# Mixture of experts on one core: thirteen groups of a heavy and one or two light experts instead of fifteen pairs, and weights fetched into idle places before the first

## The chip, the cores and the metric

The kernel runs on one core of one Trainium2 chip. The metric is the device time of one execution in microseconds (us), here the median of three runs. A profiled execution of the same program gives the rows quoted below; its span is the time from the first to the last instruction on the core.

## The reference

One decoder block on 512 tokens of 1024 values, float32: RMSNorm, projection, differential attention beside an S5 state-space branch, output projection, residual; then a mixture of 32 experts, four per token, and a final RMSNorm. What bears on the change is the mixture:

```python
def _moe(h, w_router, b_router, w1, b1, w2, b2):
    logits = (hf @ w_router + b_router).astype(jnp.float32)
    top_val, top_idx = lax.top_k(logits, TOP_K)      # 4 of 32
    gates = jax.nn.softmax(top_val, axis=-1)
...
    def expert_block(args):
        xb, e = args
        gu = xb @ w1[e] + b1[e]                      # 1024 -> 2048
        gate, up = jnp.split(gu, 2, axis=-1)
        gate = jnp.minimum(gate, SWIGLU_LIMIT)
        up = jnp.clip(up, -SWIGLU_LIMIT, SWIGLU_LIMIT)
        glu = gate * jax.nn.sigmoid(SWIGLU_ALPHA * gate)
        return ((up + 1.0) * glu) @ w2[e] + b2[e]    # 1024 -> 1024
```

The output is the sum over a token's four experts, each times its gate, added to the residual.

## The kernel before

**Weights.** Each expert has twelve chunks of 128 x 2048 float32 (1.049 MB): eight of w1 ("up") and four of w2 ("down"). All 32 experts are read once, 384 chunks. They land in seven raw tiles (three `raw2`, four `raw`, `weight_tile`), all loaded by SyncE in one fixed order (`chunks`, `chunk`, `load`), so that a load waits until the chunk seven loads earlier has been used.

**Ranks.** After routing, experts are ranked by the number of their tokens. Ranks 0 to 12 are heavy: a block of 128 rows, weights split into a high half (`hA`, by ScalarE, L926) and a low half (`hB`, by VectorE, L927), three products per weight (`up_heavy`, `down_heavy`), at most three chunks split ahead (`AHEAD`, three `hA` and three `hB` tiles). Ranks from 13 on are light: 64 rows, or 32 for the ranks in `SMALL`, multiplied straight from the raw tile in float32 (`up_light`, `down_light`). Rank 31 is a light block whose expert is always expert 0, so its weights can be loaded before routing is known; rank 0 has an extra block of 32 rows, X. The matmuls of all of these stand at L1078 (`Stream.matmul`). A block's rows are found by four slot matmuls (L975), gathered from `h2_d` in DRAM by GpSimd (L1028), and transposed by TensorE (L1050 light, L1061 heavy). The bias of a light expert is four matmuls (L1094). Between up and down TensorE transposes the gated activations (L1191 light, L1157 heavy). Results are added to `acc` by scatter matmuls (L1351), 16 for a heavy block, 8 for a light one, and VectorE's additions (L1354); a group issues those of the group before it.

**Order.** The expert stage is written as sixteen pairs. Pair 0 (`first_pair`) is ranks 31 and 13, all light. Pairs 1 to 6 and 8 to 14 are a heavy and a light expert: heavy up, light up, heavy down, light down. Pairs 7 and 15 are two light experts each (19 and 20, 26 and 27). Within `pair` the next pair's blocks are prepared (`block_of`, `prepare2`), and `later` places three pieces of other work: tables in pair 3 and the two halves of the down bias (`down_bias`, eight matmuls in all at L1300) in pairs 5 and 7.

**The start.** Chunks 0 to 6 of expert 0 are loaded long before the experts begin. Chunks 7 to 9 go into split tiles after the last write of `h2_d` (L948, kept there by `issue_after`). `out_tile` is the output projection of one quarter of the tokens: it writes x1 (L684) and h2 (L692) to DRAM. `out_weights` splits its weights into the same ring of `hA` and `hB` tiles. When all is routed, VectorE and TensorE make the table of ranks `perm`, the biases by rank `bT` (sixteen matmuls, L1246) and the list `ordi` of experts by rank (L1250, L1254), which SyncE reads (L1493) before it can load any expert but expert 0.

Of the kernel before, what the change touches and what calls it, by code (L numbers as in the profile page):

```python
# [11 lines left out]
I32 = mybir.dt.int32  # L12
# [21 lines left out]
NHEAVY = 13  # L34
SMALL = (28, 29, 30)
NRAW = 7
AHEAD = 3
# [9 lines left out]
def decoder_block_kernel(ctx: ExitStack, tc: tile.TileContext, A, out):  # L47
# [26 lines left out]

    turn_hl = dict(A=-1, B=0)
# [461 lines left out]
    wo = A['w_out'][0].rearrange("(k p) n -> p k n", p=P)  # L537
    WOH, WOL = [], []

    def out_weights():  # L540
        for kp2 in range(4):
            w = raw_tile()
            if kp2 < 2:
                SP.dma_start(w.rearrange("p (k n) -> p k n", n=D), wo[:, 2 * kp2:2 * kp2 + 2])
            else:
                for k in range(2):
                    r0 = (2 * kp2 + k) * P
                    SP.dma_start(w[:, k * D:(k + 1) * D],
                                 A['w_out'][0, r0:r0 + P].rearrange("(g c) n -> c g n", c=CW))
            wh, wl = hl_tile("A"), hl_tile("B")  # L550
            ACT.activation(wh, w, AF.Copy)
            V.tensor_tensor(wl, w, wh.bitcast(F32), op=OP.subtract)
            WOH.append(wh.rearrange("p (k n) -> p k n", n=D))
            WOL.append(wl.rearrange("p (k n) -> p k n", n=D))

# [102 lines left out]
    last_rows = [None]  # L658

    def out_tile(t):  # L660

# [201 lines left out]

    def load(eidx, c):

        w = weight_tile()
        SP.dma_start(w, w1r[eidx, c] if c < 8 else w2r[eidx, c - 8])
        return w
# [90 lines left out]
    def ps_m():  # L959
        return mp.tile([P, 512], F32, name="pm", tag="pm", bufs=2)  # L960
# [75 lines left out]
    def rows_of(B):  # L1036
# [3 lines left out]
        V.tensor_scalar(B.oT, iot, B.meta[:, 1:2], None, op0=OP.is_equal)  # L1040

    def prepare2(B):

        light, xg, n, selc = B.light, B.xg, B.n, B.selc
        if light:
            xT, B.aT = (mo.tile([P, KT * 64], F32, name=z + "Tl", tag=z + "Tl", bufs=2)[:, 0:KT * n]
                        .rearrange("p (k q) -> p k q", q=n) for z in "xa")
            pt = ps_m()
# [136 lines left out]

    def act_light(B, half, late=False):
        if B.n == 32:
            return act_small(B, late) if half == 0 else None
# [45 lines left out]
    perm = mo.tile([P, NE], F32, name="perm")  # L1234
    V.tensor_scalar(perm, iot[:, 0:NE], key[:, 2:3], None, op0=OP.is_equal)

    permr = mo.tile([P, NE], F32R, name="permr")
    V.tensor_copy(permr, perm)
    bT = mo.tile([P, 2, 2, 4, NE], F32, name="bT")
    for u in range(2):  # L1240
# [6 lines left out]
        ACT.activation(bT[:, u].rearrange("p h k r -> p (h k r)"), pb_[:, 0:256], AF.Copy)  # L1247
    po = ps_m()
    for i in range(2):
        PE.matmul(po[0:1, i * NE:(i + 1) * NE], ecol[0:32, i:i + 1], perm[0:32], start=True, stop=True)  # L1250
    orow = mo.tile([1, 2, NE], F32, name="orow")
    V.tensor_copy(orow, po[0:1, 0:64])
    ordi = mo.tile([1, NE], I32, name="ordi")
    V.tensor_copy(ordi, orow[:, 0])  # L1254
    for i in range(2):
# [227 lines left out]

    rest = iter((13, 14, 15, 16, 28, 17, 18, 19, 20, 29, 21, 22, 23, 30, 24, 25, 26, 27))
# [11 lines left out]

    chunks = [(31, c) for c in range(12)] + [(pairs[0][1], c) for c in range(12)]
    chunks += [(r, c) for h, l in pairs[1:]
               for r, cs in ((h, range(8)), (l, range(8)), (h, range(8, 12)), (l, range(8, 12))) for c in cs]
    place = {x: i for i, x in enumerate(chunks)}  # L1500
    weights = [early[c] for c in range(10)]

    def chunk(r, c):
        while len(weights) <= place[r, c]:
            z = chunks[len(weights)]
            weights.append(load(expert_id(z[0]), z[1]))
        return weights[place[r, c]]
# [5 lines left out]

    def next_pair(n):
        return pairs[n + 1] if n + 1 < len(pairs) else (None, None)

# [4 lines left out]
    def down_last(n, rl, L):  # L1521

        nh = next_pair(n)[0]
        gl = [ps_g()]
        for c in range(8, 12):
            down_light(L, c - 8, chunk(rl, c), gl)
            if nh is not None and nh < NHEAVY and c >= 9:
                split_ahead(nh, c - 9)
        return gl

    def first_pair(B):

        (rb, rl), (nh, nl) = pairs[0], pairs[1]
        nxt = {}
# [22 lines left out]

    def pair(n, B, X, L):

        (rh, rl), (nh, nl) = pairs[n], next_pair(n)  # L1560
        nxt = {}
        g = [ps_g() for _ in range(2 if B.light else 4)]
        gx = [ps_g()] if X else None
        for c in range(8):
            w = chunk(rh, c)
            if B.light:
                up_light(B, c, w, g)
            else:
                wh, wl = split(w)
                up_heavy(B, c, wh, wl, g)  # L1570
                if X:
                    up_light(X, c, w, gx)
                if c + AHEAD < 8:
                    split_ahead(rh, c + AHEAD)
            if c == 1 and nh is not None:
                nxt['h'] = block_of(nh)
            elif c == 3 and nl is not None:
                nxt['l'] = block_of(nl)
            elif c == 2 and n in later:
                later[n]()  # L1580
            elif c >= 5:
                scatter(c - 5, False)
        if B.light:
            leave_light(B, g)
        else:
            for half in range(2):
                act_heavy(B, half, g[half], g[2 + half])
        if X:
            leave_light(X, gx)
        gl = [ps_g() for _ in range(L.n // 32)]  # L1590
        for c in range(8):
            up_light(L, c, chunk(rl, c), gl)
            if c == 4:
                for half in range(2):
                    act_light(B, half) if B.light else turn_heavy(B, half)
                if X:
                    for half in range(2):
                        act_light(X, half)
            if c >= 5 and not B.light:
                split_ahead(rh, 8 + c - 5)  # L1600
        leave_light(L, gl, not B.light)
        g = [ps_g() for _ in range(1 if B.light else 2)]
        gx = [ps_g()] if X else None
        for c in range(8, 12):
            w = chunk(rh, c)
            if B.light:
                down_light(B, c - 8, w, g)
            else:
                wh, wl = split(w)
                down_heavy(B, c - 8, wh, wl, g)  # L1610
                if X:
                    down_light(X, c - 8, w, gx)
            if c == 8:
                for half in range(2):
                    act_light(L, half, not B.light)
                if not B.light:
                    split_ahead(rh, 11)
            elif c == 9:
# [9 lines left out]
        if X:  # L1628
            gated(X, gx)
        gl = down_last(n, rl, L)  # L1630
        if nh is None:
            beyond(L.last)
        gated(L, gl, nh is not None and nh < NHEAVY)
# [6 lines left out]
    for n in range(1, len(pairs)):  # L1640
        blocks = pair(n, *blocks)

# [82 lines left out]
```

## Time and profile before

| what | value |
|---|---|
| runs (us) | 1430.03, 1433.55, 1435.22; median 1433.55 |
| profiled execution | 1432.14 us, span 1430.2 us |
| mean granted TensorE clock | 0.956 of full speed |
| front, to the first expert matmul | 335.65 us |
| pair 0, to the first matmul of pair 1 | 62.65 us |
| pairs 1 to 15 | 1012.0 us |
| tail | 19.9 us |
| moved by DMA | 477.68 MB, mean 334 GB/s |

The stages are cut at the first expert matmul of each pair on TensorE, as read in the timeline. "Busy" of TensorE is modelled at the ends of matmuls, so that a stretch can be called busy in which some waiting is hidden.

### The profile page before, as it was taken

The page shows a single profiled execution, that of the slowest core. Times are in us where ns is not written, and L with a number is a line of the kernel's source. Part 1 is how long each engine was busy: PE and PEld are TensorE (multiplying, and loading weights), DVE is VectorE, ACT ScalarE, POOL GpSimd, SP SyncE. Part 2 cuts the span into 40 slices and gives each one's busy share as a digit, 9 for nine tenths or more (in the row PEclk, how much of TensorE's full clock was granted, in tenths as well). Part 3 has the DMA queues.
Part 4 walks back from the last instruction along what each step waited for, and adds up shares of the span by engine and source line. Part 5 has one row for each costly group of instructions (what it writes and reads, how often), then busy time and mean ns, then how long its engine had stood idle before and what let it go on. Part 6 is the DMA issues. An engine that isn't in the chain of part 4 may idle for free. (4 is left out here: it accounts for less than half of the span.)

```text
span 1430.2 us, 18851 instructions
## 1 busy us (share of the span) xinstructions
PE 1347.5 (94%) x6888; PEld 836.7 (59%) x6888; DVE 934.5 (65%) x1557; ACT 567.2 (40%) x681; POOL 133.1 (9%) x97
## 2 busy tenths in 40 slices
PE   3999999998999999999999999899999999999996
PEld 1778764774365656657565446565655565656532
DVE  4899546653285867778676537685867586867524
ACT  6442327321245354545254114445343354453312
POOL 1020101222010101102010000020101010201000
PEclk8999858997999999999999999999999999999998
DMA  9745647748899999999799999999997899999994
GB/s 273 245 124 195 204 148 211 254 140 321 362 400 407 361 406 366 403 379 415 307 395 367 409 393 409 417 377 388 365 401 275 346 377 383 372 394 363 416 415 176
DMA packets 103603, 477.68 MB, mean 334 GB/s; under 512 B 24739, under 2 KB 41987, under 8 KB 52307
## 3 DMA queue, kind: packets, MB, share of 16 engines
q1 hardware_dynamic: 90416, 459.86, 82.5%
q0 software_dynamic: 4432, 14.05, 2.9%
q10 hardware_dynamic: 8658, 2.52, 0.8%
q8 instruction: 56, 0.92, 0.3%
q14 instruction: 41, 0.33, 0.1%
HBM read 467.73 MB, written 8.67 MB: 333 GB/s over the span
## 5 line engine op out<-in xcount | busy, mean ns | idle before, releaser
L927 DVE TENSOR_TENSOR hB<-raw,hA 128x2048 fp32r<-128x2048 f32 x156 | 355.3, 2287 | 54.8 <-ACT hA L926 54.3
L926 ACT ACTIVATE hA<-raw 128x2048 fp32r<-128x2048 f32 x156 | 295.0, 1911 | 139.2 <-PE pg L1078 75.5
L1078 PE MATMUL pg<-raw,xTl 128*64 128x512 f32 (+1 forms) x1272 | 263.1, 600 | 0.1
L1078 PE MATMUL pg<-hA,xT 128*128 128x512 f32 x832 | 229.0, 400 | 0.0
L1078 PEld LDWEIGHTS pg<-hA,xT 128*128 128x128 f32 x832 | 157.1, 190 | 42.6 <-issue 6.0
L1028 POOL DMA_INDIRECT xg<-h_d,tid x32 | 83.1, 2596 | 874.5 <-DVE oh L971 730.7
L1078 PEld LDWEIGHTS pg<-raw,xTl 128*64 128x64 f32 (+1 forms) x1272 | 76.6, 132 | 146.5 <-issue 141.0
L1078 PE MATMUL pg<-hA,aT 128*128 128x512 f32 x416 | 139.7, 416 | 7.2 <-ACT hA L926 7.2
L1078 PE MATMUL pg<-hB,xT 128*128 128x512 f32 x416 | 126.1, 404 | 12.0 <-DVE hB L927 11.8
L1078 PE MATMUL pg<-raw,aTl 128*64 128x512 f32 (+1 forms) x752 | 127.5, 524 | 0.0
L1354 DVE TENSOR_TENSOR acc<-acc,pm 128x512 f32<-128x512 f32 x128 | 83.4, 683 | 42.0 <-PE pm L1351 41.5
L1078 PEld LDWEIGHTS pg<-hA,aT 128*128 128x128 f32 x416 | 80.1, 195 | 35.2 <-ACT hA L926 13.9
L1078 PEld LDWEIGHTS pg<-hB,xT 128*128 128x128 f32 x416 | 76.3, 190 | 36.8 <-DVE hB L927 20.1
L1078 PE MATMUL pg<-hB,aT 128*128 128x512 f32 x208 | 79.9, 411 | 5.3 <-DVE hB L927 5.3
L1078 PEld LDWEIGHTS pg<-raw,aTl 128*64 128x64 f32 (+1 forms) x752 | 41.0, 127 | 68.1 <-issue 63.4
L1351 PE MATMUL pm<-yy,oT 128*128 128x512 f32 x208 | 66.4, 408 | 1.0 <-ACT hA L926 0.4
L1141 ACT ACTIVATE gm<-gm 128x512 f32<-128x512 f32 x26 | 16.4, 631 | 124.3 <-DVE gm L1139 124.3
L1194 DVE TENSOR_TENSOR gb<-pm,bT 128x512 f32<-128x512 f32 x32 | 21.2, 688 | 63.0 <-PE pm L1191 62.2
L1162 DVE TENSOR_TENSOR aT<-pm,aT 128x512 fp32r<-128x512 f32 x26 | 16.8, 686 | 61.9 <-ACT aT L1161 61.9
L1326 ACT ACTIVATE yyl<-gy 64x512 fp32r<-64x512 f32 (+1 forms) x48 | 26.8, 559 | 70.9 <-DVE gy L1318 70.2
L1167 ACT ACTIVATE gu<-pg 128x512 f32<-128x512 f32 x36 | 20.1, 588 | 86.7 <-PE pg L1078 86.7
L1351 PE MATMUL pm<-yyl,oT 128*128 128x512 f32 (+1 forms) x152 | 51.8, 423 | 1.4 <-DVE acc L1354 0.8
(495 smaller groups left out, 1799.8 us busy)
## 6 DMA issues: line engine op xcount, KB each, us to landing
raw<-in_w_dram SPq DMA_DIRECT2D x381, 1024.0 KB, 9.4
raw<-in_w_ada_dram SPq DMA_DIRECT2D x16, 1024.0 KB, 4.8
raw<-in_w_ada_dram SPq DMA_DIRECT2D x16, 512.0 KB, 5.6
raw<-in_w_in_dram SPq DMA_DIRECT2D x8, 1024.0 KB, 6.5
xt<-in_x_dram SPq DMA_DIRECT2D x4, 512.0 KB
raw<-in_w_out_dram SPq DMA_DIRECT2D x2, 1024.0 KB
raw<-in_w_out_dram SPq DMA_DIRECT2D x4, 512.0 KB, 14.6
xh<-in_x_dram SPq DMA_DIRECT2D x4, 512.0 KB, 4.1
```

The costliest lines, as they stand in the source:

```text
L926: splits['hi'] = ACT.activation(wh, w, AF.Copy)
L927: splits['lo'] = V.tensor_tensor(wl, w, wh.bitcast(F32), op=OP.subtract)
L1028: POOL.indirect_dma_start(out=xg[0:n], out_offset=None, in_=h2_d[:, :], in_offset=bass.IndirectOffsetOnAxis(ap=tid[0:n, :1], axis=0))
L1078: ins = PE.matmul(*args, **kw)
L1141: ACT.activation(gm, gm, AF.Gelu_apprx_sigmoid)
L1162: V.tensor_tensor(lo, u4, hi.bitcast(F32), op=OP.subtract)
L1167: left = ACT.activation(gu, pss[half], AF.Copy)
L1194: biased = V.tensor_tensor(gb, p4, bT[:, :, half, :, B.rank:B.rank + 1].to_broadcast([P, 2, 4, 64]), op=OP.add)
L1326: high = ACT.activation(hi, g, AF.Copy)
L1351: PE.matmul(ps[n], oT, rows, start=(seen[n] == 1), stop=(2 * seen[n] == len(mms)))
L1354: V.tensor_tensor(acc[:, t, ns], acc[:, t, ns], ps[n], op=OP.add)
```

## The change

The expert stage becomes fourteen groups. Group 0 is as before (31 and 13). The other thirteen have one heavy expert and one light expert, and in groups 2, 4, 7 and 12 a second light expert (`TWO_LIGHT`). The order there is: heavy up, first light up, heavy down, second light up, first light down, second light down. The pairs of two light experts are gone. The second half of the down bias moves from the light pair 7 to group 8, a heavy one.

Nine chunks are fetched ahead: chunks 7 to 10 of expert 0 are issued inside the last `out_tile`, right behind its matmuls and ahead of its x1 and h2 writes; chunk 11 after routing; and the first four chunks of the expert of rank 13 go into a split tile and the places of `yy`, `xT` and `aT`, which the first heavy group uses later. For that, `out_weights` takes its four parts in the order 2, 3, 0, 1 and the turn of the split tiles is shifted. The list `ordi` is made ahead of the biases by rank, and the tile `aTl` is taken when it is filled.

```diff
+TWO_LIGHT = (2, 4, 7, 12)
...
-        for kp2 in range(4):
+        for kp2 in (2, 3, 0, 1):
...
+    def ahead(cs):
+
+        with tc.issue_after(last_rows[0].ins):
+            for c in cs:
+                early[c] = split_tile("AB"[c % 2], F32)
+                SP.dma_start(early[c], w1r[0, c] if c < 8 else w2r[0, c - 8])
...
             PE.matmul(pss[n], ml[:, k, ts], wh[:, ns], start=False, stop=(k == 3))
+        if t == NT - 1:
+            ahead(range(7, 11))
...
-    with tc.issue_after(last_rows[0].ins):
-        for c in range(7, 10):
-            early[c] = split_tile("AB"[c % 2], F32)
-            SP.dma_start(early[c], w1r[0, c] if c < 8 else w2r[0, c - 8])
+    ahead(range(11, 12))
...
-    pairs = [(r, next(rest)) for r in (31, 1, 2, 3, 4, 5, 6)]
-    pairs.append((next(rest), next(rest)))
-    pairs += [(r, next(rest)) for r in (7, 8, 9, 0, 10, 11, 12)]
-    pairs.append((next(rest), next(rest)))
+    groups = [(31, [next(rest)])]
+    for n, r in enumerate((1, 2, 3, 4, 5, 6, 7, 8, 9, 0, 10, 11, 12), 1):
+        groups.append((r, [next(rest) for _ in range(2 if n in TWO_LIGHT else 1)]))
...
+    spare = [lambda: split_tile("A", F32)]
+    spare += [lambda n=n: mo.tile([P, 2048], F32, name=n, tag=n, bufs=1) for n in ("yy", "xT", "aT")]
+    weights = [early[c] for c in range(12)]
...
+        if M:
+            g = [ps_g() for _ in range(M.n // 32)]
+            for c in range(8):
+                up_light(M, c, chunk(rm[0], c), g)
+            leave_light(M, g)
+            g = [ps_g()]
+            for c in range(8, 12):
+                down_light(L, c - 8, chunk(rl, c), g)
+                if c == 8:
+                    for half in range(2):
+                        act_light(M, half)
+            gated(L, g)
+            L, rl = M, rm[0]
         gl = down_last(n, rl, L)
...
-    later = {3: beyond_tables, 5: lambda: down_bias(0), 7: lambda: down_bias(1)}
+    later = {3: beyond_tables, 5: lambda: down_bias(0), 8: lambda: down_bias(1)}
```

SyncE's queue at the end of the front, before: the last x1 write (`x_d`) and h2 write (`h_d`), three loads of expert 0 into split tiles, the first part of `acc`, two loads into raw tiles, and the reading of `ordi`.

```order
L684 DMA x_d<-xh 128x1024
L692 DMA h_d<-t_2583 128x1024
L948 DMA hB<-in_w_dram 128x2048
L948 DMA hA<-in_w_dram 128x2048
L948 DMA hB<-in_w_dram 128x2048
L1011 DMA acc<-x_d 128x1024
L867 DMA raw_2985<-in_w_dram 128x2048
L867 DMA raw_2991<-in_w_dram 128x2048
L1493 TENSOR_LOAD ordi
```

The same place in the changed program:

```order
L665 DMA hB<-in_w_dram 128x2048
L665 DMA hA<-in_w_dram 128x2048
L665 DMA hB<-in_w_dram 128x2048
L665 DMA hA<-in_w_dram 128x2048
L693 DMA x_d<-xh 128x1024
L701 DMA h_d<-t_2583 128x1024
L665 DMA hB<-in_w_dram 128x2048
L1016 DMA acc<-x_d 128x1024
L1501 TENSOR_LOAD ordi
```

Four loads stand ahead of the two writes, one instead of three between the h2 write and `acc`, and `ordi` is read before any further load; the loads into `hA`, `yy`, `xT` and `aT` follow it.

TensorE's queue in group 2 of the changed program, from the end of the heavy down matmuls (`hA`, `hB` with `aT`) to the second light's up and the first light's down (raw tiles with `xTl` and `aTl`); L1085 is the former L1078, L1057 the former L1050, L1200 the former L1191, L980 the former L975:

```order
L1085 MATMUL pg<-hA,aT 128x512 x2
L1057 MATMUL pm<-ident,xg 128x32 x8
L1085 MATMUL pg<-raw,xTl 64x512 x16
L1085 MATMUL pg<-raw_4213,xTl 64x512 x4
L1085 MATMUL pg<-raw_4219,xTl 64x512 x4
L1085 MATMUL pg<-raw_4225,xTl 64x512 x4
L1085 MATMUL pg<-raw,xTl 64x512 x4
L1200 MATMUL pm<-ident,gu 128x128 x8
L980 MATMUL pm<-tb,oh 128x66
L1085 MATMUL pg<-raw,aTl 64x512 x4
```

Before, light down matmuls followed the heavy down ones at once; now eight chunks of the second light's up stand between, with its transposes behind them.

VectorE's queue before the first heavy group, before: `sel` is the bias selector of that group, `ms` and `tid` the slots of a later block, L927 the low half.

```order
L1065 TENSOR_TENSOR xT<-pm,xT 128x512
L1054 TENSOR_SCALAR sel<-ones,perm 128x128
L977 COPY ms<-pm 128x66
L971 TENSOR_SCALAR oh<-iot,posr 128x128
L979 CAST tid<-ms 128x1
L1406 TENSOR_TENSOR meta<-ms 128x1
L1032 COPY meta<-ms 128x1
L971 TENSOR_SCALAR oh<-iot,posr 128x128 x3
L927 TENSOR_TENSOR hB<-raw_3185,hA 128x2048
```

And in the changed program, where L936 is the low half, L1327 and L1338 the gate products of the light expert:

```order
L1072 TENSOR_TENSOR xT<-pm,xT 128x512
L936 TENSOR_TENSOR hB<-raw_3184,hA 128x2048
L936 TENSOR_TENSOR hB<-raw_3194,hA 128x2048
L936 TENSOR_TENSOR hB<-raw,hA 128x2048
L1327 SCALAR_TENSOR_TENSOR gy<-pg,meta,g2l 128x512
L1061 TENSOR_SCALAR sel<-ones,perm 128x128
L1338 TENSOR_TENSOR yyl<-gy,yyl 64x512 x2
```

Three low halves have moved ahead of the selector and of the slots of the next blocks.

## Rows read from the trace of the kernel before

**Rows 1.** The page: busy time and share of an engine, and the weights' queue.
```profile
PE 1347.5 (94%) x6888; PEld 836.7 (59%) x6888; DVE 934.5 (65%) x1557; ACT 567.2 (40%) x681; POOL 133.1 (9%) x97
...
q1 hardware_dynamic: 90416, 459.86, 82.5%
```

**Rows 2.** Windows of five pairs (2, 5, 7, 8, 15).
```profile
core 0: us, PE busy (x) PEld busy (x) DVE busy (x) ACT busy (x) POOL busy (x), PEclk, DMA share, GB/s
...
464.30:532.20 67.90, 66.63 (x311) 42.42 (x310) 49.02 (x65) 30.53 (x27) 5.37 (x2) 1.00 0.96 382
...
662.90:738.50 75.60, 73.48 (x320) 44.12 (x317) 53.01 (x73) 33.10 (x31) 8.31 (x2) 0.98 0.90 359
...
804.90:869.40 64.50, 63.25 (x285) 24.62 (x281) 29.77 (x75) 11.87 (x17) 3.83 (x4) 1.00 0.99 398
869.40:934.60 65.20, 57.87 (x333) 40.05 (x332) 44.70 (x60) 31.79 (x26) 0.94 (x1) 0.95 1.01 417
...
1353.00:1410.30 57.30, 55.76 (x242) 20.60 (x238) 20.92 (x39) 6.54 (x12) 0.00 (x0) 1.00 0.88 364
```

**Rows 3.** TensorE's largest wait from 664 to 1410 us: total, times, longest.
```profile
PE pg L1078 <- DVE hB L927: 11.1, 9, 2.1
```

**Rows 4.** Waits of SyncE's queue, whole span.
```profile
SPq L867 <- PE pg L1078: 485.4, 225, 18.7
```

**Rows 5.** A window of 5 us at the start (columns as in rows 2).
```profile
310.00:315.00 5.00, 4.70 (x27) 3.76 (x25) 2.73 (x4) 1.62 (x4) 1.29 (x1) 1.00 0.00 0
```

**Rows 6.** Timeline at the start: start, duration, engine, line, operation, [wait].
```profile
319.46 0.32 SPq L692 DMA_DIRECT2D h_d<-t  x1
...
325.04 1.06 POOL L1028 DMA_INDIRECT xg<-h_d,first_id  x1 [7.06 <-DMA hB<-in_w_dram]
...
328.22 2.73 PE L1246 MATMUL pm<-permr,b1t 64*128 64x32 f32 x16 [0.93 <-DVE permr L1238]
...
333.65 1.08 PE L1050 MATMUL pm<-ident,xg 64*128 64x64 f32 x8 [2.39 <-DMA xg<-h_d,first_id]
...
335.65 1.97 PE L1078 MATMUL pg<-raw,xTl 128*64 128x512 f32 x2
```

**Rows 7.** Timeline around the start of pair 1: ScalarE, then TensorE.
```profile
395.14 1.91 ACT L926 ACTIVATE hA<-raw 128x2048 fp32r<-128x2048 f32 x1 [1.91 <-DMA raw<-in_w_dram]
...
400.60 2.08 PE L1078 MATMUL pg<-hB,xT 128*128 128x512 f32 x4 [1.06 <-DVE hB L927]
```

**Rows 8.** TensorE's timeline in the last light pair.
```profile
1354.82 1.19 PE L1351 MATMUL pm<-yy,oT 128*128 128x512 f32 x4
1355.85 0.78 PE L1351 MATMUL pm<-yyl,oT 128*128 128x512 f32 x2
...
1373.71 13.95 PE L1078 MATMUL pg<-raw,xTl 128*64 128x512 f32 x64
1387.60 1.57 PE L1191 MATMUL pm<-ident,gu 128*128 128x128 f32 x8
...
1392.79 7.21 PE L1078 MATMUL pg<-raw,aTl 128*64 128x512 f32 x32
```

**Rows 9.** TensorE's timeline at the end of pair 1.
```profile
455.53 0.71 PE L1050 MATMUL pm<-ident,xg 64*128 64x64 f32 x8
...
463.19 0.74 PE L1094 MATMUL pg<-b1t,sel 64*128 64x512 f32 x4
463.86 0.63 PE L975 MATMUL pm<-tb,oh 128*128 128x66 f32 x4
```

**Rows 10.** TensorE's timeline: the second down bias in pair 7.
```profile
807.21 0.61 PE L1285 MATMUL pm<-ident,Gt 128*32 128x128 f32 x4
...
811.33 3.88 PE L1300 MATMUL pm<-b2r,GT 32*128 32x512 f32 x8
```

**Rows 11.** TensorE's timeline at the start of pair 5.
```profile
666.22 1.62 PE L1078 MATMUL pg<-hB,xT 128*128 128x512 f32 x4 [2.12 <-DVE hB L927]
```

**Rows 12.** TensorE's timeline at the start of the tail.
```profile
1413.91 3.22 PE L1656 MATMUL pg<-acc,ident 128*128 128x512 f32 x4 [3.60 <-DMA fgb<-in_final_g_dram]
```

More of the change, by code (lines that the diff above doesn't have):

```diff
@@ L1235, in decoder_block_kernel @@
     V.tensor_scalar(perm, iot[:, 0:NE], key[:, 2:3], None, op0=OP.is_equal)
+    po = ps_m()
+    for i in range(2):
+        PE.matmul(po[0:1, i * NE:(i + 1) * NE], ecol[0:32, i:i + 1], perm[0:32], start=True, stop=True)
+    orow = mo.tile([1, 2, NE], F32, name="orow")
+    V.tensor_copy(orow, po[0:1, 0:64])
+    ordi = mo.tile([1, NE], I32, name="ordi")
+    V.tensor_copy(ordi, orow[:, 0])
     permr = mo.tile([P, NE], F32R, name="permr")
@@ L1494, in expert_id @@
         return eids[r]
-    chunks = [(31, c) for c in range(12)] + [(pairs[0][1], c) for c in range(12)]
-    chunks += [(r, c) for h, l in pairs[1:]
-               for r, cs in ((h, range(8)), (l, range(8)), (h, range(8, 12)), (l, range(8, 12))) for c in cs]
+    up, down = range(8), range(8, 12)
+    chunks = [(r, c) for r in (31, groups[0][1][0]) for c in range(12)]
+    for h, (l, *m) in groups[1:]:
+        chunks += [(r, c) for r, cs in [(h, up), (l, up), (h, down)] + [(r, up) for r in m] + [(l, down)]
+                   + [(r, down) for r in m] for c in cs]
     place = {x: i for i, x in enumerate(chunks)}
-    weights = [early[c] for c in range(10)]
+    spare = [lambda: split_tile("A", F32)]
+    spare += [lambda n=n: mo.tile([P, 2048], F32, name=n, tag=n, bufs=1) for n in ("yy", "xT", "aT")]
+    weights = [early[c] for c in range(12)]
     def chunk(r, c):
@@ L1531, in first_pair @@
     def first_pair(B):
-        (rb, rl), (nh, nl) = pairs[0], pairs[1]
+        (rb, (rl,)), (nh, nl) = groups[0], next_group(0)
         nxt = {}
@@ L1556, in first_pair, with group @@
         return nxt['h'], None, nxt['l']
-    def pair(n, B, X, L):
-        (rh, rl), (nh, nl) = pairs[n], next_pair(n)
+    def group(n, B, X, L):
+        (rh, (rl, *rm)), (nh, nl) = groups[n], next_group(n)
         nxt = {}
-        g = [ps_g() for _ in range(2 if B.light else 4)]
+        g = [ps_g() for _ in range(4)]
         gx = [ps_g()] if X else None
+        M = None
+        at = dict(h=2, l=6) if rm else dict(h=1, l=3)
         for c in range(8):
             w = chunk(rh, c)
[L1566 to L1578, printed above, removed]
+            wh, wl = split(w)
+            up_heavy(B, c, wh, wl, g)
+            if X:
+                up_light(X, c, w, gx)
+            if c + AHEAD < 8:
+                split_ahead(rh, c + AHEAD)
+            if rm and c == 0:
+                M = block_of(rm[0])
+            elif rm and c == 5:
+                prepare2(M)
+            if nh is not None and c in at.values():
+                z = 'h' if c == at['h'] else 'l'
+                nxt[z] = block_of(nh if z == 'h' else nl)
             elif c == 2 and n in later:
                 later[n]()
-            elif c >= 5:
+            if c >= 5:
                 scatter(c - 5, False)
[L1583 to L1587, printed above, removed]
+        for half in range(2):
+            act_heavy(B, half, g[half], g[2 + half])
         if X:
@@ L1594, in pair @@
                 for half in range(2):
[L1595 removed]
+                    turn_heavy(B, half)
                 if X:
@@ L1598, in pair @@
                         act_light(X, half)
-            if c >= 5 and not B.light:
+            if c >= 5:
                 split_ahead(rh, 8 + c - 5)
-        leave_light(L, gl, not B.light)
-        g = [ps_g() for _ in range(1 if B.light else 2)]
+        leave_light(L, gl, True)
+        g = [ps_g() for _ in range(2)]
         gx = [ps_g()] if X else None
@@ L1629, in pair @@
             gated(X, gx)
+        if M:
[7 more added lines that the diff above has]
+                if c == 8:
+                    for half in range(2):
+                        act_light(M, half)
+            gated(L, g)
+            L, rl = M, rm[0]
         gl = down_last(n, rl, L)
@@ L1632, in pair @@
             beyond(L.last)
-        gated(L, gl, nh is not None and nh < NHEAVY)
+        gated(L, gl, nh is not None)
         if nh == 0:
@@ L1636, in pair @@
         return nxt.get('h'), nxt.get('x'), nxt.get('l')
-    later = {3: beyond_tables, 5: lambda: down_bias(0), 7: lambda: down_bias(1)}
+    later = {3: beyond_tables, 5: lambda: down_bias(0), 8: lambda: down_bias(1)}
     blocks = first_pair(first)
-    for n in range(1, len(pairs)):
-        blocks = pair(n, *blocks)
+    for n in range(1, len(groups)):
+        blocks = group(n, *blocks)
     fgb = mo.tile([P, D], F32, name="fgb", tag="aT", bufs=1)
```

53 lines of the change are left out of this document (22 added, 31 removed).

## The prediction

> **What bounds the kernel now.** I read the page's shares first. TensorE is busy for 94% of the span, and the queue that brings the weights takes 82.5% of the sixteen DMA engines' time [rows 1]. Either can be the bound, and an average does not say where, so I cut the expert stage at the first matmul of each pair and read one window per pair [rows 2]. Three kinds of pair come out. An ordinary pair (heavy with a 64-row light expert) has TensorE busy for 66.63 of its 67.90 us while the DMA share is 0.96: TensorE ends last. A pair with a 32-row light expert has TensorE busy for 57.87 of 65.20 us while the queue runs flat out at 417 GB/s: there the weights end last. At 417 GB/s a chunk of 1.049 MB takes 2.51 us, so 24 chunks are 60.4 us. A pair of two light experts lies between: 63.25 of 64.50 us busy at share 0.99, 55.76 of 57.30 us at 0.88.
>
> The view of waits agrees: from 664 to 1410 us TensorE's largest wait is 11.1 us, for the low halves [rows 3]. SyncE, which issues the loads, stood 485.4 us behind TensorE's use of the raw tiles [rows 4]: the loads mostly wait for free tiles, not the tiles for loads.
>
> The start is another regime. From 310 to 315 us nothing moves on the wire [rows 5]; then three loads follow the last h2 write, the gather of the first expert's rows is issued at 325.04, and its transposes start at 333.65, released by that DMA [rows 6]. Before the first ordinary pair ScalarE's high halves wait for weights (1.91 us before the one at 395.14) and TensorE waits 1.06 us for a low half at 400.60 [rows 7].
>
> **The change, part by part.**
>
> *Two pairs go.* The light-light pairs take 64.50 and 57.30 us [rows 2]: -121.8 us.
>
> *Four second lights come.* Their price is read in the last light-light pair, where TensorE has no gap [rows 8]. The 64 up matmuls run from 1373.71 to 1387.60 (13.89), the eight transposes take 1.57, the 32 down matmuls take 7.21. The transposes of the gathered rows take 0.71, the bias matmuls 0.74, the slot matmuls 0.63 [rows 9]. Scatter: four matmuls start 1.03 us apart from the next group [rows 8], so 0.26 each, and a light block has eight: 2.1. Together 26.8 us, four times 107.2. Nothing hides these, since TensorE is what ends last beside them. The other bound is the wire: 12 x 2.51 plus a gather, an estimate of 0.6 us for its 0.26 MB at that rate, is 30.7 us each, 122.8 for four. I take the first: a two-light group moves 36 chunks (90.4 us and 1.8 of gathers) against 67.9 + 26.8 = 94.7 us of TensorE.
>
> *The second down bias moves* out of a light-light pair into a heavy group: its matmuls and transposes are 3.88 + 0.61 [rows 10], +4.5 us, as nothing covers TensorE there. The pair that already had the other bias took 75.60 us, 7.7 more than an ordinary one [rows 2], but it also started late behind a 32-row expert (below), so 4.5 is taken and 7.7 kept as the bound.
>
> *Scatters change hosts.* Each group scatters the blocks of the group before. The group after the removed middle pair scatters a heavy and a light block (24 matmuls) where it had two lights (16): +2.1. The last group's heavy block has its 16 scatter matmuls behind the last expert matmul: 4.1 us. There TensorE waits 3.60 us for the final norm's weights today [rows 12], which may cover all but 0.5; VectorE's additions behind them and the start of the tail's sums after them are not sure to be covered, so I take +3. The last heavy group in turn prepares nobody: two slot sets (1.26), the row transposes of a light (0.71) and of a heavy block (about as many): -2.5.
>
> *Two-light groups behind 32-row experts.* Three of the four follow a group that the wire bounds, and start with few loaded chunks. What that costs is seen once: in the pair that started at 662.90 the first low half came 2.12 us late [rows 11], and 75.60 - 67.90 less the bias of 4.5 leaves 3.2 us for such a start in all. These starts exist before too; what the longer light phases add I set at +1 each, +3, between 0 and 3 x 3.2.
>
> *The start.* Four chunks are issued before the last x1 and h2 writes, while the wire is idle [rows 5], and one instead of three stands before the gather. The gather took 8.6 us beside three loads; alone with one I expect it by 330. Then the sixteen bias matmuls (328.22 to 330.95 [rows 6]), now behind the four of the rank table, end last at about 331.4, and the first up matmul follows 2 us later as now (333.65 to 335.65): 333.4, so -2.2. The first light experts' own matmuls are not bound by loads (five chunks more in place change nothing there), but the next loads start earlier by the chunks fetched ahead. The high halves of the first heavy group no longer wait, and three low halves now stand on VectorE ahead of the gate products. So the 1.06 at the first low half goes, and of the waits of ScalarE the last full one (1.91) [rows 7], together about -2.8. Start together -5, from 0 to -8. Beyond that the nine chunks in idle places (22.6 us of wire) are worth nothing, as TensorE works through both light experts on data that is there.
>
> Here a rule speaks against the change. The Trainium skill ("DMA: Bandwidth & Descriptors", section "Issuing engines are not separate DMA queues") states that transfers started by any engine run on the same sixteen DMA engines and interleave. The trace agrees (8.6 us for a gather of 0.26 MB beside loads). By it the x1 and h2 writes behind four loads get slower, which is the fourth rival.
>
> **The sum.** -121.8 + 107.2 + 4.5 + 2.1 + 3 - 2.5 + 3 - 5 = -9.5 us. The profiled execution took 1432.14 us (span 1430.2), so it would take 1422.6; the median of the runs shown stands 1.4 above it, which gives 1424.0. I say 1423.
>
> **The rivals.**
>
> *Nothing comes of it (0.25).* TensorE's work is the same in both programs. By busy time the light-light pairs leave only 1.25 + 1.54 us idle [rows 2], and the new starts take 3 back. For it: no gaps in [rows 8]. Against it: some of that busy time is waiting, since the terms above explain only 116 of the 121.8 (four lights at 23.4, the 24 scatter matmuls of each heavy pair before and 8 of a light, the bias, 3.5 of preparation). With half of the start's gain it is -2.8 + 3 - 2.5 = -2.3, 1430 us.
>
> *Slower by an empty store (0.12).* Seven raw tiles hold 17.6 us of transfers. A two-light group's last 16 chunks (40.2 us on the wire) are used in about 31 us. If the store is not full when the second light starts, that light runs at 30.7 us instead of 26.8, and the next heavy group starts like the one in [rows 11], 3.2 us late. Four times 7.1 is 28 us: 1451. It decides as soon as loads lose more than about 2.5 us of a two-light group (94.7 - 92.2). For it: the full queue beside an idle TensorE in the 32-row pair. Against it: in ordinary pairs 7.5 us of wire time are left over (67.9 - 60.4), so the store refills. With half of it, 1437, no change.
>
> *More than forecast (0.13).* The 32-row pair shown leaves 7.33 us of TensorE idle [rows 2], and there are three such pairs. If the steadier mix lets loads run ahead through them and a third of 22 us goes, and the start gives 8 instead of 5, the sum is -20: 1413. The Trainium skill ("Perfetto Trace Analysis", section "Optimization Strategy") says that a kernel whose most-contended engine changes between regimes may gain by interleaving them. The trace shows such regimes (a wire share of 0.99 and 1.01 in some windows, 0.96 with TensorE full in others). By it this would be the likeliest case.
>
> *A later start (0.10).* Four loads are 10 us of wire. If their tiles come free only late in the empty window of [rows 5], at 313 say, they move until 323, h2's last part, written now at 319.46 [rows 6], lands up to 3.5 us later, and so does the first gather: +3.5 instead of -5, 1431 us. If they go by 309 they are through when it is written.
>
> **How the numbers follow.** The forecast has 0.40; its own range, from the bounds of bias, tail, start and group starts, is 1415 to 1430. Half a per cent is 7.2 us, about what a measurement of this kernel can tell from no change, so faster begins below 1426.4 and slower above 1440.7. Faster: three quarters of the forecast and a little more (0.33), the third rival (0.13), and a share of the first where the start gives its full gain (0.08): 0.54. Slower: 0.10 of the second and 0.02 of mishaps beside it: 0.12. Same: the rest, 0.34. Eight in ten lie between 1408 and 1438: under 1408 would need the third rival and more, above 1438 the second in full.
>
> **What the profile after would show.** The four two-light groups take 92 to 96 us each, with TensorE busy for over 0.97 and no wait at the second light's first up matmul. The group with the second bias takes about 72 to 76. The wire is busy between 309 and 320 us, the first gather is used near 331, and the first up matmul stands near 333.4. The first heavy group shows no wait for a low half. I am wrong if the second light's up chunks show gaps (weights late), if the groups after the two-light ones begin with waits and a lower granted clock, or if the first up matmul does not move or moves later.

## The result and the profile after

The changed kernel took 1455.65 us (median of 3 runs, 1453.71 to 1456.47) against 1433.55: a ratio of 1.0156, 95% interval 1.0122 to 1.0190. It is slower by 22 us where about 10 us less was forecast. The profiled execution has a span of 1454.6 us.

The page's shares hardly tell it. TensorE is as busy as before [rows 1], in a longer span:

```profile
PE 1351.4 (93%) x6888; PEld 844.2 (58%) x6888; DVE 925.9 (64%) x1541; ACT 568.7 (39%) x681; POOL 118.5 (8%) x97
...
q1 hardware_dynamic: 90416, 459.86, 81.5%
```

TensorE's waits from the first expert on do (330 to 1435 us). This is the first line of the view of waits before (what waited, for what: total us, times, longest); the low halves head it, as in [rows 3]:

```profile
engine line waited for: us in total, times, longest us
PE pg L1078 <- DVE hB L927: 17.2, 15, 2.1
```

These are its first three lines after. A wait stands above the low halves that was not in the view before:

```profile
PE pm L1057 <- DMA xg<-h_d,tid: 23.9, 4, 6.7
PE pg L1085 <- DVE hB L936: 12.5, 13, 1.6
PE pg L1085 <- ACT hA L935: 12.1, 6, 3.1
```

L1057 is the transposing of a light block's gathered rows (L1050 before), and it waits four times: once in each two-light group. The timeline of TensorE at the start of group 2 shows where (start, duration, line, tiles, and in brackets the wait that ended there):

```profile
462.08 0.53 PE L980 MATMUL pm<-tb,oh 128*128 128x66 f32 x4
462.87 1.20 PE L1085 MATMUL pg<-hB,xT 128*128 128x512 f32 x4 [0.26 <-DVE hB L936]
463.91 2.02 PE L1085 MATMUL pg<-hA,xT 128*128 128x512 f32 x8
470.56 0.67 PE L1057 MATMUL pm<-ident,xg 64*128 64x64 f32 x7 [4.62 <-DMA xg<-h_d,tid]
471.15 2.07 PE L1085 MATMUL pg<-hB,xT 128*128 128x512 f32 x4
473.03 2.68 PE L1085 MATMUL pg<-hA,xT 128*128 128x512 f32 x8
...
477.34 2.02 PE L1085 MATMUL pg<-hA,xT 128*128 128x512 f32 x8
```

GpSimd had issued the second light's gather here:

```profile
460.64 2.96 POOL L1033 DMA_INDIRECT xg<-h_d,tid  x1 [48.88 <-DVE oh L976]
```

The transposes need it at 465.9 and get it at 470.5. Behind them in the same queue stand the heavy expert's matmuls, whose weights are there. They start late, and the first ones run slowly (four in 2.07 us, eight in 2.68, against eight in 2.02 before and after). The windows of 5 us show what goes with that second part: the granted clock (the column before the DMA share) falls to 0.91 in the window in which TensorE stands, and is 0.75 in the one after, between its two levels of 2.4 and 1.2 GHz:

```profile
462.00:467.00 5.00, 3.67 (x18) 2.63 (x16) 5.00 (x12) 1.64 (x2) 4.20 (x2) 1.00 1.00 418
467.00:472.00 5.00, 1.44 (x9) 1.26 (x10) 4.91 (x4) 2.80 (x3) 0.00 (x0) 0.91 1.02 342
472.00:477.00 5.00, 5.00 (x17) 3.67 (x17) 0.94 (x2) 1.05 (x2) 0.00 (x0) 0.75 1.03 420
477.00:482.00 5.00, 5.00 (x24) 4.05 (x23) 1.91 (x2) 3.32 (x3) 0.00 (x0) 1.00 0.58 241
```

The windows by group (columns as in rows 2) show pair 0, the four two-light groups (2, 4, 7, 12), the group with the second bias (8), the last group and the tail:

```profile
336.50:393.20 56.70, 54.17 (x257) 21.11 (x256) 19.31 (x55) 14.81 (x20) 3.70 (x4) 0.96 0.91 336
...
457.90:560.80 102.90, 96.67 (x444) 55.05 (x444) 57.09 (x110) 31.37 (x33) 8.27 (x5) 0.98 0.92 367
...
627.60:730.30 102.70, 94.24 (x425) 52.66 (x425) 55.70 (x85) 33.23 (x35) 9.54 (x4) 0.93 0.91 361
...
868.50:971.20 102.70, 93.01 (x426) 51.75 (x425) 55.70 (x86) 33.25 (x35) 9.58 (x4) 0.95 0.93 369
971.20:1047.50 76.30, 75.10 (x324) 47.18 (x324) 52.35 (x64) 34.49 (x29) 0.90 (x1) 0.96 0.91 362
...
1263.70:1364.90 101.20, 94.34 (x424) 52.34 (x424) 53.53 (x73) 33.24 (x35) 8.16 (x3) 0.95 0.92 367
1364.90:1430.60 65.70, 64.26 (x283) 40.32 (x284) 45.29 (x45) 27.56 (x23) 0.00 (x0) 1.00 0.84 344
1430.60:1454.60 24.00, 11.20 (x32) 5.12 (x32) 15.77 (x29) 6.22 (x14) 2.64 (x4) 0.92 0.30 111
```

So the 24.4 us between the spans of the two profiles (1454.6 and 1430.2) divide into three: the first heavy group starts 5.1 us earlier (393.2 against 398.3), the thirteen groups take 1037.4 us where the fifteen pairs took 1012.0 (+25.4), and the tail takes 4.1 more (24.0 against 19.9). The two-light groups alone take 409.5 us; the forecast had 92 to 96 each.

### The profile page after: what moved, and what is told of

Same layout as the page of the kernel before. It is cut to its first block, busy times and chain, and to the rows that moved or that the text cites. A ratio compares the mean times of both kernels' runs of the same rounds, so it can differ in the third digit from the quotient of the medians.

```text
span 1454.6 us, 18825 instructions
## 1 busy us (share of the span) xinstructions
PE 1351.4 (93%) x6888; PEld 844.2 (58%) x6888; DVE 925.9 (64%) x1541; ACT 568.7 (39%) x681; POOL 118.5 (8%) x97
## 5 line engine op out<-in xcount | busy, mean ns | idle before, releaser
L936 DVE TENSOR_TENSOR hB<-raw,hA 128x2048 fp32r<-128x2048 f32 x156 | 355.4, 2288 | 99.5 <-ACT hA L935 98.8
L1085 PE MATMUL pg<-raw,xTl 128*64 128x512 f32 (+1 forms) x1240 | 251.3, 596 | 0.0
L1085 PE MATMUL pg<-hA,xT 128*128 128x512 f32 x832 | 241.5, 407 | 5.7 <-ACT hA L935 5.6
L1085 PEld LDWEIGHTS pg<-hA,xT 128*128 128x128 f32 x832 | 160.4, 194 | 53.0 <-ACT hA L935 9.2
L1085 PEld LDWEIGHTS pg<-raw,xTl 128*64 128x64 f32 (+1 forms) x1240 | 75.2, 131 | 143.7 <-issue 138.9
L1085 PE MATMUL pg<-hB,xT 128*128 128x512 f32 x416 | 137.4, 418 | 7.2 <-DVE hB L936 7.1
L1085 PE MATMUL pg<-hA,aT 128*128 128x512 f32 x416 | 137.4, 410 | 6.5 <-ACT hA L935 6.5
L1033 POOL DMA_INDIRECT xg<-h_d,tid x32 | 68.5, 2140 | 890.4 <-DVE oh L976 667.2
L1085 PE MATMUL pg<-raw,aTl 128*64 128x512 f32 (+1 forms) x736 | 123.7, 522 | 0.4 <-DMA raw<-in_w_dram 0.4
L1363 DVE TENSOR_TENSOR acc<-acc,pm 128x512 f32<-128x512 f32 x112 | 72.9, 684 | 44.5 <-PE pm L1360 44.2
L1085 PEld LDWEIGHTS pg<-hA,aT 128*128 128x128 f32 x416 | 78.9, 192 | 34.3 <-ACT hA L935 11.7
L1085 PEld LDWEIGHTS pg<-hB,xT 128*128 128x128 f32 x416 | 80.1, 198 | 31.9 <-DVE hB L936 13.0
L1085 PE MATMUL pg<-hB,aT 128*128 128x512 f32 x208 | 79.2, 408 | 5.4 <-DVE hB L936 5.4
L1085 PEld LDWEIGHTS pg<-raw,aTl 128*64 128x64 f32 (+1 forms) x736 | 39.8, 127 | 67.8 <-issue 61.4
L1335 ACT ACTIVATE yyl<-gy 64x512 fp32r<-64x512 f32 (+1 forms) x48 | 26.8, 558 | 74.0 <-DVE gy L1327 73.3
L1168 ACT ACTIVATE aT<-pm 128x512 fp32r<-128x512 f32 x26 | 14.2, 594 | 95.9 <-PE pm L1164 95.9
L1085 PEld LDWEIGHTS pg<-hB,aT 128*128 128x128 f32 x208 | 39.6, 192 | 15.9 <-DVE hB L936 7.6
```

What stands on the lines that cost most here:

```text
L936: splits['lo'] = V.tensor_tensor(wl, w, wh.bitcast(F32), op=OP.subtract)
L1033: POOL.indirect_dma_start(out=xg[0:n], out_offset=None, in_=h2_d[:, :], in_offset=bass.IndirectOffsetOnAxis(ap=tid[0:n, :1], axis=0))
L1085: ins = PE.matmul(*args, **kw)
L1168: ACT.activation(hi, u4, AF.Copy)
L1335: high = ACT.activation(hi, g, AF.Copy)
L1363: V.tensor_tensor(acc[:, t, ns], acc[:, t, ns], ps[n], op=OP.add)
```

## The experiments

Twelve kernels were run, each timed against the kernel before. Two theories stood against each other: that the wait for the second light's gathered rows makes the loss (A), or that the second light's weights come late because the raw tiles are empty (B). Single executions of one kernel lie up to some 20 us apart, so ratios with intervals decide, and windows of one profile are used for stages inside the groups. The kernel before was timed again each time: its median was 1431.14 us beside e1 to e4, 1434.34 beside f1 to f4, and 1433.67 beside f5, g2, g4 and g5. A difference in us between runs timed apart is therefore loose by some 3 us, and the ratios are the better measure.

### Is it the gather's wait or late weights

**e1.** One step of the changed kernel moved: the second light's rows are transposed during the first light's up matmuls.

```diff
-            elif rm and c == 5:
-                prepare2(M)
...
             if c >= 5:
                 split_ahead(rh, 8 + c - 5)
+            if M and c == 6:
+                prepare2(M)
```

> The changed kernel with one step moved: the row transposes of the second light expert are prepared during the first light expert's up matmuls instead of during the heavy ones. Theory A (in the two-light groups TensorE stands in its queue behind these transposes, which wait for the gather, 6 us each time and 1 to 2 us of lower clock after it): the four groups fall from 102 us to about 94 to 96 each, the wait for the gathered rows (23.9 us in all) goes, time 1424 to 1430 us. Theory B (the second light's weights come late because the raw tiles are empty): the wait only moves, the groups stay at 100 or more, time 1450 to 1456.

Measured: 1434.14 us, ratio 1.0007 (0.9982 to 1.0032). That is 21.5 us less than the changed kernel, by one step moved. The wait for gathered rows is gone from the view, whose first line is now the one of the low halves:

```profile
PE pg L1085 <- DVE hB L936: 15.0, 16, 1.6
```

The gather is issued as early as before (460.03) and the transposes come at 496.08, without a wait:

```profile
460.03 2.96 POOL L1033 DMA_INDIRECT xg<-h_d,tid  x1 [46.48 <-DVE oh L976]
...
496.08 0.71 PE L1057 MATMUL pm<-ident,xg 64*128 64x64 f32 x8
```

The four two-light groups fell to 95.49, 95.65, 94.38 and 92.31 us:

```profile
457.33:552.82 95.49, 94.69 (x444) 53.63 (x444) 56.65 (x110) 31.31 (x33) 8.27 (x5) 1.00 0.99 391
552.82:621.28 68.46, 61.04 (x342) 42.25 (x343) 48.07 (x61) 33.72 (x27) 0.90 (x1) 0.95 1.00 413
621.28:716.93 95.65, 92.82 (x422) 51.35 (x420) 54.56 (x80) 31.44 (x34) 9.23 (x3) 0.96 0.95 379
...
858.57:952.95 94.38, 90.30 (x422) 49.34 (x420) 54.44 (x80) 31.23 (x34) 9.23 (x3) 1.00 0.98 393
952.95:1027.71 74.76, 73.63 (x324) 46.37 (x325) 52.34 (x64) 34.49 (x29) 0.91 (x1) 0.98 0.92 369
...
1247.30:1339.61 92.31, 91.90 (x420) 50.09 (x418) 51.96 (x65) 31.34 (x34) 8.16 (x2) 0.99 0.97 387
```

That is 31.7 us off these groups: the 23.9 of waiting and 7.8 that went with it. The granted clock is part of the 7.8 (0.98, 0.93, 0.95 and 0.95 in the four groups after, 1.00, 0.96, 1.00 and 0.99 in e1); how much was not separated. Not all of it was a gain: the other nine groups together took 6.6 us more (634.5 against 627.9), the three 32-row groups alone 7.3 (203.6 against 196.3). Group 3 is one: 68.46 us at a wire share of 1.00. Why is not shown: it could be that the loads ran ahead while TensorE stood, but taking loads away (f4, below) did not shorten these groups. Theory A is shown for this wait. But the time stopped at that of the kernel before, 4 to 10 us above what was expected, so the forecast failed in more than this wait.

**e4.** In the changed kernel half of the second lights' up weights are not loaded, each even chunk is used twice.

```diff
+    seconds = {r for _, ls in groups for r in ls[1:]}
+    chunks = [(r, c) for r, c in chunks if not (r in seconds and c < 8 and c % 2)]
...
-                up_light(M, c, chunk(rm[0], c), g)
+                up_light(M, c, chunk(rm[0], c - c % 2), g)
```

> The changed kernel with half of the second lights' up weights left out: of eight chunks only the even ones are loaded, each is used twice. TensorE's work is the same, the wire carries 16 chunks (40 us) less. Theory A (gather): no change beyond 3 us, 1452 to 1458, the waits for gathered rows stay. Theory B (empty store): most of the 33 us beyond the forecast goes, 1422 to 1432.

Measured: 1446.66 us, ratio 1.0099 (1.0070 to 1.0129). Theory B asked for 1422 to 1432 and does not hold alone: the waits for gathered rows stay as they were, with the wire relieved of 40 us.

```profile
PE pm L1057 <- DMA xg<-h_d,tid: 25.0, 4, 7.0
```

But 9 us went (8 by the ratios), which theory A had not expected; TensorE's waits for high halves fell from 12.1 us to 5.7. Late weights cost something of their own, beside the gather.

**f4.** The same on top of e1.

> The late-prepared version (e1) with half of the second lights' up weights left out: only the even chunks are loaded, each is used twice. With the gather's wait gone, this shows what the wire alone still costs: if the groups are bound by TensorE, within 3 us of e1 (1431 to 1437); if the store of chunks runs empty behind the two-light groups, 8 to 14 us less, 1420 to 1426, and it is the 32-row groups that become shorter.

Measured: 1420.72 us, ratio 0.9921 (0.9894 to 0.9948), 13 us less than e1 (12 by the ratios). The wire does bind in part. The place was expected wrongly: the 32-row groups kept their length (202.1 us together against 203.6), and the two-light groups themselves became shorter, 369.3 us against 377.8, as in group 7:

```profile
851.61:942.43 90.82, 89.36 (x422) 49.52 (x420) 53.27 (x73) 33.82 (x36) 8.29 (x2) 1.00 0.94 369
```

### The start

**e3.** The pairs of before with the new start alone (the hunks on `turn_hl`, `out_weights`, `ahead`, `spare` and `ordi` of the change, no group).

> The kernel before, its fifteen pairs unchanged, with the new start alone (early loads, idle places, order of the output weights, list of ranks first). Theory: 5 us less than before, 1427 to 1430 us, all of it ahead of the first heavy matmul. Rival: the loads ahead of the h2 write and the gather cost as much as they save, 1432 to 1436.

Measured: 1427.99 us, ratio 0.9967 (0.9940 to 0.9994). The gain is there, and of about the size forecast: 0.33% is 4.7 us, and the interval reaches from 0.9 to 8.6.

**e2.** The changed kernel's groups with the start of before:

```diff
-    turn_hl = dict(A=0, B=2)
+    turn_hl = dict(A=-1, B=0)
...
-        if t == NT - 1:
-            ahead(range(7, 11))
...
-    ahead(range(11, 12))
+    ahead(range(7, 10))
...
-    weights = [early[c] for c in range(12)]
+    spare = []
+    weights = [early[c] for c in range(10)]
```

> The changed kernel's groups with the start of before: chunks 7 to 9 after the last h2 write, nothing fetched into idle places, the output weights in the old order; the list of ranks still ahead of the biases. If the new start gains what the two traces show (first heavy matmul 5.1 us earlier), this takes 1459 to 1462 us. If the later h2 write (2.3 us) belongs to the new start and is given back, 1456 to 1459. If the prefetch harms, under 1455.

Measured: 1469.99 us, ratio 1.0262 (1.0226 to 1.0298), 14 us more than the changed kernel and 8 above the highest expectation. In the profiles its first heavy group starts 5.5 us later (398.7 against 393.2) and its groups take 1042.4 us against 1037.4. The start is a part of the 14; where the rest comes from was not settled.

**g5.** e1 without the idle places (`spare = []`), with the five early chunks.

> The late-prepared version (e1) with the five chunks of expert 0 fetched early, but nothing into idle places: the second expert's first four chunks are loaded into the raw tiles in their turn. If the waits at the first heavy group are removed by the idle places, that group starts 2 to 3 us later than in e1 after its first up matmul, 1436 to 1438; if the early chunks alone do it, within 1 us.

Measured: 1435.24 us, ratio 1.0004 (0.9984 to 1.0023), no change from e1 within a few us. Nothing measurable hangs on the four chunks in the places of `yy`, `xT`, `aT` and the split tile.

### The smaller terms

**f5.** e1 without the second half of the down bias.

```diff
-    later = {3: beyond_tables, 5: lambda: down_bias(0), 8: lambda: down_bias(1)}
+    later = {3: beyond_tables, 5: lambda: down_bias(0)}
```

> The late-prepared version (e1) with the second half of the down bias left out altogether. Group 8 took 74.8 us in e1 where the ordinary group 9 took 68.6. By the forecast's term (its own matmuls and transposes) e1 less 4.5 us, 1429 to 1430, and group 8 at 70; if the whole difference to an ordinary group is the bias's, less 6 to 7.5 us, 1426 to 1428, and group 8 at 67 to 68.

Measured: 1426.97 us, ratio 0.9950 (0.9932 to 0.9968), 7.2 us less than e1 (8.2 by the ratios), the upper of the two expectations, though the intervals leave room for the lower one. Group 8 takes 67.38 us:

```profile
956.01:1023.39 67.38, 66.25 (x306) 42.39 (x306) 47.43 (x50) 34.53 (x29) 0.00 (x0) 1.00 0.99 403
```

The group ahead of it takes 1.8 us more than in e1 (96.2 against 94.4), so groups 7 and 8 together are 5.6 us shorter, nearer to the bias's own 4.5.

**f1.** e1 with the two halves of the bias in groups 6 and 11, those of 32-row experts.

```diff
-    later = {3: beyond_tables, 5: lambda: down_bias(0), 8: lambda: down_bias(1)}
+    later = {3: beyond_tables, 6: lambda: down_bias(0), 11: lambda: down_bias(1)}
```

> The late-prepared version (e1) with the two halves of the down bias moved into groups 6 and 11, those of 32-row experts, where the windows show TensorE idle for 4.5 to 6 us beside a full wire. If TensorE's idle time there can hold them, the groups that lose them fall from 75 to 68 us and the others grow by under 2 each: 9 to 14 us less than e1, 1420 to 1426. Rival: the small groups grow by what the others lose, 1432 to 1436.

Measured: 1434.09 us, ratio 0.9996 (0.9970 to 1.0021), no change. The groups that lost the bias went from 75.2 and 74.8 to 68.5 and 67.4 us, the others from 66.5 and 68.6 to 70.0 and 73.4: more than half came back. TensorE's idle time in a group bound by the wire was not free room for it.

**g2.** e1 with the last heavy block's scatter between the last light's down matmuls.

```diff
             if nh is not None and c >= 9:
                 split_ahead(nh, c - 9)
+            if nh is None:
+                scatter(c - 8, c == 11)
...
     def beyond(after):
-        for i, t in enumerate((3, 2, 0, 1)):
-            scatter(t, i == NT - 1)
```

> The late-prepared version (e1) with the last heavy block's scatter matmuls put between the last light expert's down matmuls instead of behind them. In e1 they stand alone for 6.0 us, paced by VectorE's additions. Under the light matmuls they cost TensorE about 4, so 2 to 3 us less than e1, and the tail behind the last expert matmul shrinks from 25.7 to about 20.

Measured: 1432.20 us, ratio 0.9990 (0.9972 to 1.0008). 1.9 us less than e1 by the medians, inside the intervals. In the profile the tail fell from 25.7 to 20.0 us and the last group grew from 66.0 to 70.2. In e1 the sixteen matmuls had stood behind the last light, four at a time, each four held by VectorE's additions:

```profile
1405.52 1.20 PE L1360 MATMUL pm<-yy,oT 128*128 128x512 f32 x4
1407.03 1.33 PE L1360 MATMUL pm<-yy,oT 128*128 128x512 f32 x4 [0.32 <-DVE acc L1363]
1408.54 1.33 PE L1360 MATMUL pm<-yy,oT 128*128 128x512 f32 x4 [0.18 <-DVE acc L1363]
1410.06 1.32 PE L1360 MATMUL pm<-yy,oT 128*128 128x512 f32 x4 [0.18 <-DVE acc L1363]
```

### What the best versions reach

**f2.** f1 with the light experts in another order: no 32-row expert behind a two-light group, the last group with two lights. (The expectation also says that none is followed by one; group 11 is, by group 12.)

```diff
-TWO_LIGHT = (2, 4, 7, 12)
+TWO_LIGHT = (4, 8, 12, 13)
...
-    rest = iter((13, 14, 15, 16, 28, 17, 18, 19, 29, 20, 21, 22, 23, 24, 30, 25, 26, 27))
+    rest = iter((13, 14, 28, 15, 16, 17, 18, 29, 19, 20, 21, 22, 23, 30, 24, 25, 26, 27))
```

> As f1, with another order of the light experts: two second lights in groups 4, 8, 12 and 13, the 32-row experts in groups 2, 6 and 11, so that none of them follows a two-light group and none is followed by one. If a two-light group empties the store of chunks and the small group behind it pays (in e1 the groups 2 and 3 ran at wire shares 0.99 and 1.00), the small groups fall back from 66 to 69 us to 63 to 66: 5 to 9 us less than f1. Rival (the wire's total decides, wherever the lights stand): within 3 us of f1.

Measured: 1426.41 us, ratio 0.9963 (0.9934 to 0.9991), 7.7 us less than f1 by the medians, as expected. By the ratios it is 4.7, and the intervals overlap, so the gain is not sure. The expected place does not bear it out: the three 32-row groups took 68.0, 70.9 and 72.7 us against 69.0, 70.0 and 73.4, and all groups together 1015.0 against 1009.2. The tail was 3.3 us shorter. The rest lies ahead of the groups, where profiles of kernels with the same front scatter by more than that.

**g4.** f2 with the edit of g2.

> The order of f2 (32-row experts away from two-light groups, bias in their groups, last group with two lights) with the same move of the last scatter. f2 measured 1426.4; its tail is 22.0 us: 1 to 2 us less, 1424 to 1426, which would be the fastest of all versions.

Measured: 1428.12 us, ratio 0.9958 (0.9942 to 0.9973), 1.7 us above f2 where 1 to 2 us less was expected; the two cannot be told apart.

**f3.** The pairs of before with the new start (e3), and the bias in pairs 8 and 12.

> The old pairs with the new start (e3), and the down bias in the pairs of 32-row experts (8 and 12). If grouping itself is worth nothing, this is as good as f1 or better: e3 less 7 to 11 us, 1417 to 1421. If the groups are worth something beyond the bias, f1 or f2 is faster than this.

Measured: 1430.41 us, ratio 0.9967 (0.9944 to 0.9990), the same as e3 where 7 to 11 us less was expected. The bias in the 32-row pairs gained nothing here either.

The best grouped versions (0.9958, 0.9963) and the pairs with nothing but the new start (0.9967) cannot be told apart. What is gained is the start; the grouping gains nothing that these runs can measure. In e1, which has the same start as e3, it costs: the two were timed together, and their medians are 1434.14 and 1427.99 us, their ratios 0.4% apart, with intervals that just overlap.

## Why the prediction was wrong

**The step that failed** is "Four second lights come". It priced the second light as TensorE's own work (26.8 us each) and the gather as time on the wire (0.6 us), and read the transposes' 0.71 us from a row in which the gathered rows had long been there [rows 9]. It did not ask when they arrive at their new place. There the gather is asked for at the group's start, its rows land 8 to 10 us later, and TensorE's queue reaches the transposes 1 to 5 us behind the request. The first gather's own row, 8.6 us from issue to use, had shown that size [rows 6]; it was used for the start alone. The trace of the kernel before had it for all of them, in its view of DMA issues (out<-in, queue, operation, count, median us from issue to landing):

```profile
xg<-h_d,tid POOLq DMA_INDIRECT x32, 10.2
```

None of the four rivals named this wait, and the signs listed at the end would have shown only that the groups are too long. The runs put it at 31.7 us within the two-light groups and 21.5 us in the time (e1).

**The bare price of a second light came out, in part by luck.** Without the wait the four groups take 377.8 us in e1. Four ordinary groups at 67.9 and four lights at 26.8 are 378.8. But 2.1 of each 26.8 is scatter, most of which the group behind issues (groups 5 and 8 of e1 have 32 scatter matmuls, the ordinary group 9 has 24), so only some 371 were due within the four. Near that is f4, with the same matmuls and 40 us less on the wire: 369.3. About 8 us of these groups in e1 hang on the loads, which the forecast had put at 3 there.

**What else was left of the forecast** is read from e1, which should have come to 1423 (the sum itself gives 1424.0) and came to 1434. By stages its span is 1.1 us above before: start -5.0, groups +0.3, tail +5.8. Three places of the sum were too small.
- The groups: their terms (the sum without start and tail) come to -7.5, and +0.3 came. Groups 3, 6 and 11 took 203.6 us where the pairs with the same light experts took 196.5, +7.1. Of this +5.2 is group 3, behind a two-light group, about 2 of it the scatter just named; +1.3 is group 6, where +2.1 for scatter was allowed. Group 8, behind a two-light group as well, began with a wait of 2.5 us. Late starts (+3) had been looked for at the two-light groups alone; they come behind them too. And the -2.5 of the last group did not show: 66.0 us against 64.8 in pair 14.
- The second bias: 4.5 forecast, 7.2 by the timed f5, of which the profile of groups 7 and 8 bears 5.6. The bound of 7.7 held by the medians.
- The tail: +3 forecast, 4.1 in the changed kernel and 5.8 in e1. The additions do set the pace, 1.5 us for each four matmuls; the wait for the final weights [rows 12], which was to cover them, is no longer there, but another of 2.2 us is.

**The start was right in size, not in its make-up.** -5 forecast, -4.7 by e3 (0.9 to 8.6). That the profile after has -5.1 as well is luck: in the eleven profiles with the whole new start the first heavy group begins between 388.8 us (e4) and 403.7 (e3), in the two with the old one at 398.3 and 398.7. As forecast, the wire was busy from 310 to 320 us (shares 0.98 and 1.03), and the first heavy group shows no wait for a low half. But h2's last part was written at 321.75 instead of 319.46 [rows 6] (the whole front ran 2.3 us later, since before the output projection and so not by the loads ahead of that write), and the first up matmul stood at 336.45, not at 333.4: later than before, which was named as a sign of being wrong. In the eleven profiles it lies between 332.0 and 342.4, so one profile does not decide it. The gather took 5.8 us from issue to use instead of 8.6, with one load ahead of it instead of three; the fourth rival, a later start by the shared engines, is not what e3 shows. In the profile after, the 5 us lie in pair 0, which took 56.8 us (336.45 to 393.24) instead of 62.7, at a granted clock of 0.96 instead of 0.89. In the profiles with the whole new start it took 56.8 to 61.4 us, in the two with the old one 62.7 and 63.3; where the clock was as low as before (0.88 in e3, 61.4 us) only 1.3 us of the gain is left there. How much of the 5 us is the clock's was not settled.

**The rivals.** "Nothing comes of it" (0.25) is nearest to what the grouping is worth once the wait is away: e1's ratio of 1.0007 holds the start's gain as well, and against e3, the pairs with that start, e1 is about 6 us slower; f2 and g4 are level with e3. "Slower by an empty store" gave the nearest time (1451), for a reason that is only a part: taking 40 us off the wire gains 9 us with the gather's wait (e4) and 13 without it (f4). "More than forecast" did not come: the Trainium skill ("Perfetto Trace Analysis", section "Optimization Strategy") says that interleaving regimes with different busiest engines may gain. None of these runs shows that gain: with the transposes out of the way the wire share rose to 0.99 and 1.00 in groups 2 and 3 of e1, so the regimes were merged there, and the time stayed.

## What to carry to other kernels

When a change creates work in a new place, price the arrival of every operand there, gathers included, and not only the engine time of the instructions: transposes of 0.7 us held everything behind them in TensorE's queue for 4.6 to 6.7 us, as long as their rows were late. So for each new consumer on the engine that bounds the kernel, take the issue of its transfer and the landing time from the trace, and compare them with its place in the queue; moving such a consumer behind work that is ready (e1) took back 21.5 of the 22 us. And when a forecast is compared stage by stage, each term has to be booked in the stage that issues its work, or two errors can cancel, as the scatter and the late weights did in the two-light groups.

## What was not expected of the hardware

- A stall of 4.6 us cost TensorE more than 4.6 us: the granted clock fell to 0.91 and 0.75 in the two windows of 5 us, and the next four matmuls took 2.07 us where four took 1.20 before the stall. Over four groups 23.9 us of waiting came to 31.7.
- The gathers of the four second lights (64 rows of 4 KB each) took 7.8 to 9.9 us from issue to use, and all 33 gathers after, of 32 to 128 rows, 8.9 us to landing by the median (4.3 to 14.0). At the wire's 417 GB/s the bytes of 64 rows are under a microsecond. Halving the second lights' up loads (e4) left TensorE's wait for them as it was (25.0 us).
- The stretch from the first expert to the first heavy group took 56.8 to 61.4 us in kernels with the same instructions there, with granted clocks of 0.96 to 0.88: one profile of a start proves little, and the timed e3 alone bears the gain.
